# Block sums made in memory, two planner reserves, and adaptive sums by one-column products, in a planned two-layer decoder trunk

## The chip, the core and the metric

The kernel runs on one core of one Trainium2 chip. The metric is device time in microseconds (us) of one execution, the median of several. The engines are named as in the profile: PE is TensorE's matmuls, PEld its weight loads, DVE is VectorE, ACT is ScalarE, POOL is GpSimd, SP is SyncE, which here issues nearly all plain DMAs. POOL issues the DMAs that accumulate.

## The reference

Two layers of a hybrid decoder trunk on one sequence of 1024 tokens and 1024 channels, in float32, and a final RMSNorm:

```python
c_act = jax.nn.silu(c)
for l in range(DEPTH):
    ada = c_act @ w_ada[l] + b_ada[l]
    shift, scale, gate = jnp.split(ada, 3, axis=-1)
    h = rmsnorm(x, norm_g[l]) * (1.0 + scale[:, None, :]) + shift[:, None, :]
    p = h @ w_in[l]
    ...
    y = jnp.concatenate([y_m, y_r], axis=-1) @ w_out[l]
    x = x + gate[:, None, :] * y
return rmsnorm(x, final_g)
```

What stands at the "..." splits `p` among eight heads of 256 channels, four mLSTM heads (`y_m`) and four retention heads (`y_r`), each computed chunk by chunk and normalised. Two things matter for this change. The adaptive sums `c_act @ w_ada[l]` are products of one row of 1024 numbers with a 1024 x 3072 matrix. And `w_out` is 2048 x 1024: the kernel multiplies by it with seven block products in place of eight, for which it needs sums of blocks of `w_out` and of the heads' outputs.

## The kernel before

**A plan made at build time.** The program is first recorded as a list of operations on named buffers (`Program.record`), each with an assumed duration (`Program.cost`). Then `Program.simulate` plays it through: it takes the operations of each engine by due times, gives buffers to slots of their class, and lets DMAs go through one server one after another. `Program.order` does this for eight rounds, moves due times between them, and keeps the shortest plan. The final order of every engine's instructions, and which slot each buffer has, comes from there; on the chip each engine works through its own queue in that order and waits for semaphores. A reserve in the plan is time that the planner adds between two operations because the real time of one varies: `LATE` (1.5 us) after a DMA's landing for whoever uses it, `FAR` (5.0 us) in its place for buffers of the classes `q`, `kk`, `st` and `dm`.

**Numbers.** Every product of the large matrices is made of three TensorE matmuls on a high and a low float32r part (`mm3`: high x high, high x low, low x high). ACT makes the high part by a cast (`wH`, `hH`), DVE the low part by a subtraction (`wL`, `hL`). The weights' parts live in class `h`, which has nine slots of 128 x 512.

**The beginning (`beginning`).** SP loads, in an order that is pinned: half of `x` (eight tiles), then for each quarter `g` of the first layer's channels eight tiles `araw` of `w_ada` (128 rows of it, 256 columns each of shift and scale), with weights of the border in between, and the other half of `x` after the fourth quarter. `norm_rows` squares and scales the rows of `x`, TensorE transposes them (`pa<-ident,x`), and the result is copied to `xT`. `ada_part(g)` makes the adaptive sums of a quarter: TensorE multiplies the first `araw` tile by one column of `cact` (four products, one for each 128 columns), DVE multiplies the other seven by their column of `cact` and adds them into `aacc`, and TensorE adds up the partitions of `aacc` by four products with a column of ones, into the same bank. `finish_gsh` turns the bank into gain and shift, `gsh`; with these, `affine` makes `hH`, `hf` and `hL` of two tiles of `xT`, and the border's first products can run on them (`border_columns` on two column blocks, 512 columns a matmul, and `value_products`, 264 columns).

**The sums of blocks.** `weight_sums(l)` makes, for each of eight rows of blocks, four sums of two, three or four blocks of `w_out`: T1 = block 11 + 12, T2 = T1 + 22, T4 = T2 + 21, T3 = 12 + 22 (with the first digit for the half of the rows, the second for the half of the columns). It loads a block into a tile `fx` of class `h`, lets a DMA of POOL add the next block to it, stores the tile to `wdr`, adds again, and stores again. `early_job` and `late_job` do the same with the heads' outputs in `ydr`, into `fdr`. They are generators: one step of each is recorded after each pair of projections. `wdr` and `fdr` are read in `output`.

## Time and profile before

| | |
|---|---|
| median of three runs | 2096.32 us (2096.01 to 2097.2) |
| the profiled execution, its own time | 2095.88 us |
| its span, from the first to the last instruction | 2094.2 us |
| mean granted TensorE clock | 0.994 |
| DMA engines' mean use, HBM traffic | 229 GB/s, 322.16 MB read and 156.27 MB written |

The largest groups of the page, with their count, busy time, mean time of one, and the idle time of the engine just before them with what ended it:

```profile
L2068 PE MATMUL pp<-hH,wH 128*128 128x512 f32 x2416 | 958.2, 397 | 5.1 <-ACT hH L2068 2.8
L2068 PEld LDWEIGHTS pp<-hH,wL 128*128 128x128 f32 x2416 | 454.4, 188 | 106.9 <-DVE wL L2068 5.5
L2068 ACT CAST wH<-raw 128x512 fp32r<-128x512 f32 x515 | 315.5, 618 | 379.5 <-PE pp L2068 224.2
L2068 DVE TENSOR_TENSOR wL<-raw,wH 128x512 fp32r<-128x512 f32 x522 | 355.5, 685 | 106.6 <-ACT wH L2068 41.1
L2068 POOL DMA_DIRECT2D fx<-in_w_out_dram x64 | 56.7, 886 | 592.7 <-DMA wdr<-fx 188.8
```

All instructions have one line, L2068, since one loop at the end emits them in the planned order; so groups are told apart by their tiles. A matmul's duration here reaches into the next one (they are pipelined): what one costs is the distance from its start to the next one's. A fp32 product of one column, as the program writes it, shows as two matmuls.

### The profile page before, as it was taken

The numbers are of one execution on the slowest core, as the hardware profiler recorded it, in microseconds if no ns is written. First come the engines' busy times: TensorE is split into PE (matmuls) and PEld (weight loads), VectorE is DVE, ScalarE is ACT, GpSimd is POOL, SyncE is SP. The second block draws the span as 40 slices with busy tenths as digits, with TensorE's granted clock in tenths as the row PEclk, the third lists the DMA queues.
The fourth block names the chain that finished last, engine by engine and source line by source line (L and its number), as shares of the span: only waits on it lengthen the run. The fifth ranks groups of instructions, "written<-read, shape, count | busy, mean of one in ns | idle before, by whom it ended". The sixth has DMA issues, their size and how long they took to land.

```text
span 2094.2 us, 31188 instructions
## 1 busy us (share of the span) xinstructions
PE 2051.9 (98%) x9821; PEld 1705.8 (81%) x9821; DVE 1812.2 (87%) x3483; ACT 1139.4 (54%) x2124; POOL 206.1 (10%) x254
## 2 busy tenths in 40 slices
PE   6999999999999999999999999999999999999997
PEld 6888888778888888888888888888888888888886
DVE  7999999998887888894989989898978788888677
ACT  6755555456444444564666555566654434446544
POOL 0011110101001011011001000111010101110001
PEclk8999999999999999999999999999999999999999
DMA  9248676979796888999734699877768878989994
GB/s 302 80 138 222 186 214 177 254 229 265 228 269 191 246 257 233 272 318 339 231 117 117 174 238 256 232 219 202 228 195 241 232 227 226 271 250 301 333 319 149
DMA packets 508913, 480.55 MB, mean 229 GB/s; under 512 B 230706, under 2 KB 345146, under 8 KB 508748
## 3 DMA queue, kind: packets, MB, share of 16 engines
q1 hardware_dynamic: 493772, 451.29, 70.3%
q0 software_dynamic: 14976, 27.27, 7.9%
q8 instruction: 77, 1.26, 0.3%
q14 instruction: 88, 0.72, 0.1%
HBM read 322.16 MB, written 156.27 MB: 228 GB/s over the span
## 4 chain that ended last, share of the span: by engine, by line
PE 71%; DVE 13%; DMA 10%; issue 2%; SPq 2%; ACT 1%; POOL 0%; DVEq 0%; ACTq 0%; POOLq 0%
PE pp L2068 59%; PE pa L2068 12%; DVE wL L2068 3%; DVE acc L2068 2%; DVE x L2068 2%; DMA wdr<-fx 2%; SPq L2068 2%; DMA araw<-in_w_ada_dram 2%; DMA raw<-in_w_in_dram 1%; DVE raw L2068 1%; DVE rt L2068 1%; DMA fx<-in_w_out_dram 1%; DMA kk<-qdr 1%; DMA fdr<-fx 1%; DMA fx<-ydr 1%
## 5 line engine op out<-in xcount | busy, mean ns | idle before, releaser
L2068 PE MATMUL pp<-hH,wH 128*128 128x512 f32 x2416 | 958.2, 397 | 5.1 <-ACT hH L2068 2.8
L2068 PE MATMUL pp<-hL,wH 128*128 128x512 f32 x2416 | 957.0, 396 | 1.0 <-DVE hL L2068 1.0
L2068 PE MATMUL pp<-hH,wL 128*128 128x512 f32 x2416 | 955.4, 395 | 2.1 <-DVE wL L2068 1.9
L2068 PEld LDWEIGHTS pp<-hH,wL 128*128 128x128 f32 x2416 | 454.4, 188 | 106.9 <-DVE wL L2068 5.5
L2068 PEld LDWEIGHTS pp<-hH,wH 128*128 128x128 f32 x2416 | 454.4, 188 | 105.2 <-ACT wH L2068 2.9
L2068 PEld LDWEIGHTS pp<-hL,wH 128*128 128x128 f32 x2416 | 454.4, 188 | 101.6 <-DVE hL L2068 1.5
L2068 ACT CAST wH<-raw 128x512 fp32r<-128x512 f32 x515 | 315.5, 618 | 379.5 <-PE pp L2068 224.2
L2068 DVE TENSOR_TENSOR wL<-raw,wH 128x512 fp32r<-128x512 f32 x522 | 355.5, 685 | 106.6 <-ACT wH L2068 41.1
L2068 DVE SCALAR_TENSOR_TENSOR acc<-x,cols,acc 128x1024 f32<-128x1024 f32 x96 | 122.5, 1276 | 0.9 <-ACT acc L2068 0.7
L2068 POOL DMA_DIRECT2D fx<-in_w_out_dram x64 | 56.7, 886 | 592.7 <-DMA wdr<-fx 188.8
L2068 POOL TENSOR_TENSOR rsd<-va,mhalf 128x2 f32<-128x2 f32 x64 | 59.5, 930 | 562.1 <-DVE va L2068 494.4
L2068 PE MATMUL pa<-cf,q 128*128 128x258 f32 (+1 forms) x384 | 104.9, 380 | 1.9 <-DVE cf L2068 1.0
L2068 ACT ACTIVATE nd<-nd,nmu,rsd 128x256 f32<-128x256 f32 x117 | 65.3, 595 | 55.2 <-DVE nmu L2068 54.5
L2068 DVE TENSOR_TENSOR raw<-raw,raw 128x512 f32<-128x512 f32 x136 | 92.8, 684 | 0.6
L2068 PEld LDWEIGHTS pa<-q,kk 128*128 128x128 f32 x512 | 75.3, 191 | 8.7 <-issue 0.9
L2068 PEld LDWEIGHTS pa<-cf,q 128*128 128x128 f32 x384 | 69.1, 190 | 13.9 <-issue 1.8
L2068 PE MATMUL pa<-q,kk 128*128 128x128 f32 (+1 forms) x512 | 79.5, 301 | 0.5 <-DMA kk<-qdr 0.5
L2068 ACT CAST wH<-s 128x512 fp32r<-128x512 f32 x68 | 42.1, 619 | 67.7 <-PE pp L2068 35.0
L2068 DVE TENSOR_TENSOR hL<-yf,hH 128x512 fp32r<-128x512 f32 x90 | 60.7, 685 | 16.9 <-ACT hH L2068 15.3
L2068 ACT ACTIVATE yg<-yg,cols 128x512 f32<-128x512 f32 x63 | 45.5, 723 | 54.1 <-DVE yg L2068 53.5
L2068 PE MATMUL pa<-v,sd 128*128 128x258 f32 (+1 forms) x160 | 62.8, 393 | 2.1 <-ACT sd L2068 1.1
L2068 ACT CAST hH<-yf 128x512 fp32r<-128x512 f32 x89 | 53.6, 617 | 12.5 <-DMA yf<-fdr 4.9
(252 smaller groups left out, 2921.1 us busy)
## 6 DMA issues: line engine op xcount, KB each, us to landing
raw<-in_w_in_dram SPq DMA_DIRECT2D x280, 256.0 KB
araw<-in_w_ada_dram SPq DMA_DIRECT2D x96, 256.0 KB
fx<-in_w_out_dram POOLq DMA_DIRECT2D x64, 256.0 KB, 5.3
wdr<-fx SPq DMA_DIRECT2D x64, 256.0 KB
qdr<-acc SPq DMA_DIRECT2D x32, 512.0 KB
kk<-qdr SPq DMA_DIRECT2D x64, 256.0 KB
q<-qdr SPq DMA_DIRECT2D x64, 256.0 KB
ndr<-zt SPq DMA_DIRECT2D x128, 128.0 KB
```

The costliest lines, as they stand in the source:

```text
L2068: getattr(engines[op.eng], op.fn)(*[real(v) for v in op.a], **{n: real(v) for n, v in op.k.items()})
```

## The change

Three things are changed.

- The sums of blocks are made in memory: `sum_of` copies one block to its place in `wdr` or `fdr` (a DMA of SP, from memory to memory), and a DMA of POOL accumulates the other onto it there. T2 starts from a copy of T1, T4 from a copy of T2. Tiles `fx` are gone. `cost` now takes a DMA's size from its first operand where no operand is in SBUF.
- Two reserves: loads of wide `yg` tiles (class `X`) count as `far`; and a slot of class `h` is given away `LATE` after the end of a DMA among its users.
- `ada_part` makes the sums of the first two quarters from all eight `araw` tiles by products of one column, without `aacc`; the other two quarters stay as they were.

```diff
@@ record @@
-        op.far = isinstance(out, Ref) and out.buf.cls in ("q", "kk", "st", "dm")
+        op.far = isinstance(out, Ref) and (out.buf.cls in ("q", "kk", "st", "dm") or out.buf.name[:2] == "yg" and out.buf.cls == "X")
@@ cost @@
-            o = next(x for x in refs if not x.buf.dram)
+            o = next((x for x in refs if not x.buf.dram), refs[0])
...
+            k_accum = op.k.get("accum_op") is not None
...
+            if k_accum:
+                op.serve *= 1
@@ simulate @@
-                    slot_free[b.slot] = slot_last[b.slot].end
+                    slot_free[b.slot] = max(u.end + (self.LATE if u.bytes and b.cls == "h" else 0.0) for u in b.users)
@@ early_job @@
-            t = new("h", 512, "fx")
-            Q.dma_start(t, y_source(k, 0))
-            add_on(t, k, 1, "T1", k)
+            sum_of(fdr["T1"][k], y_source(k, 0), y_source(k, 1))
@@ late_job @@
-            t, u = (new("h", 512, "fx") for _ in range(2))
-            Q.dma_start(t, fdr["T1"][k])
-            Q.dma_start(u, y_source(k, 1))
-            add_on(t, k + KT, 1, "T2", k)
-            add_on(u, k + KT, 1, "T3", k)
-            add_on(t, k + KT, 0, "T4", k)
+            sum_of(fdr["T2"][k], fdr["T1"][k], y_source(k + KT, 1))
+            sum_of(fdr["T3"][k], y_source(k, 1), y_source(k + KT, 1))
+            sum_of(fdr["T4"][k], fdr["T2"][k], y_source(k + KT, 0))
@@ weight_sums @@
+    def sum_of(dst, one, two):
+
+        Q.dma_start(dst, one)
+        G.dma_start(dst, two, accum_op=ALU.add)
+
     def weight_sums(l):
         for k in range(KT):
-            for chain_ in (((None, 0, 0), ("T1", 0, 1), ("T2", 1, 1), ("T4", 1, 0)), ((None, 1, 1), ("T3", 0, 1))):
-                t = new("h", 512, "fx")
-                for name, kh, half in chain_:
-                    src = w_source(l, k + KT * kh, half)
-                    if name:
-                        G.dma_start(t, src, accum_op=ALU.add)
-                        Q.dma_start(wdr[name][k], t)
-                        yield
-                    else:
-                        Q.dma_start(t, src)
+            d = {n: wdr[n][k] for n in wdr}
+            for name, one, two in (("T1", w_source(l, k, 0), w_source(l, k, 1)), ("T2", d["T1"], w_source(l, k + KT, 1)),
+                                   ("T4", d["T2"], w_source(l, k + KT, 0)), ("T3", w_source(l, k, 1), w_source(l, k + KT, 1))):
+                sum_of(d[name], one, two)
+                yield
@@ ada_part @@
-            acc = new("F", 512, "aacc")
+            straight = (KT, KT, 1, 1)[g]
...
-            for i in range(4):
-                PE.matmul(pt[:, i:i + 1], raws[0][:, i * P:(i + 1) * P], cact[:, 0:1], start=i == 0, stop=False,
-                          skip_group_check=True)
-            ada_acc(acc, raws[1:], 1)
...
+            for kk in range(straight):
+                for i in range(4):
+                    PE.matmul(pt[:, i:i + 1], raws[kk][:, i * P:(i + 1) * P], cact[:, kk:kk + 1], start=kk == 0 and i == 0,
+                              stop=kk == KT - 1 and i == 3, skip_group_check=True)
+            if straight < KT:
+                acc = new("F", 512, "aacc")
+                ada_acc(acc, raws[straight:], straight)
+                for i in range(4):
+                    PE.matmul(pt[:, i:i + 1], acc[:, i * P:(i + 1) * P], ones, start=False, stop=i == 3,
+                              skip_group_check=True)
```

Since a planner sets the order, the diff alone does not tell where instructions stand. The first place is TensorE's queue near the first large matmul of the beginning (`pp<-hH,wH`, the border's columns on the first quarter). Of the kernel before, behind the transposes of `x`:

```order
L2068 MATMUL pa_251<-ident_74,rows_79 128x32
L2068 MATMUL pp_144<-ones_72,aacc_154 128x1 x4
L2068 MATMUL pp_294<-cact_113,araw_162 128x1 x4
L2068 MATMUL pp_326<-hH_314,wH_215 128x512
L2068 MATMUL pp_326<-hL_332,wH_215 128x512
L2068 MATMUL pp_326<-hH_314,wL_244 128x512
L2068 MATMUL pp_347<-hH_314,wH_235 128x512
L2068 MATMUL pp_294<-ones_72,aacc_260 128x1 x4
L2068 MATMUL pp_358<-cact_113,araw_253 128x1 x4
```

Of the change, at the same place; `pp_142` is the first quarter's bank, `pp_327` the second's, `pp_407` the third's:

```order
L2065 MATMUL pp_142<-cact_111,araw_134 128x1 x4
L2065 MATMUL pp_327<-cact_111,araw_162 128x1 x4
L2065 MATMUL pp_327<-cact_111,araw_169 128x1 x4
L2065 MATMUL pp_327<-cact_111,araw_178 128x1 x4
L2065 MATMUL pp_327<-cact_111,araw_185 128x1 x4
L2065 MATMUL pp_327<-cact_111,araw_197 128x1 x4
L2065 MATMUL pp_327<-cact_111,araw_211 128x1 x4
L2065 MATMUL pp_327<-cact_111,araw_221 128x1 x4
L2065 MATMUL pp_327<-cact_111,araw_233 128x1 x4
L2065 MATMUL pp_407<-cact_111,araw_265 128x1 x4
L2065 MATMUL pp_418<-hH_340,wH_226 128x512
L2065 MATMUL pp_418<-hL_352,wH_226 128x512
```

All products of the second quarter, and the first of the third, have moved ahead of the first large matmul; the eight groups of the first quarter stand ahead of these rows, among the transposes. The second place is SP's queue at the end of the border's first half, where `bv` (the value projection) is stored to `v0dr`. Of the kernel before:

```order
L2068 DMA raw_612<-in_w_in_dram 128x512
L2068 DMA v0dr_815<-bv_800 128x512
L2068 DMA v0dr_831<-bv_812 128x512
L2068 DMA raw_836<-in_w_in_dram 128x512
L2068 DMA raw_843<-in_w_in_dram 128x512
```

Of the change (`wdr<-in_w_out` is a copy of a block of `w_out`, `wdr<-wdr` a copy of a sum on which the next one builds):

```order
L2065 DMA wdr_806<-in_w_out_dram 128x512
L2065 DMA wdr_846<-wdr_642 16x4096
L2065 DMA wdr_863<-wdr_648 16x4096
L2065 DMA v0dr_878<-bv_854 128x512
L2065 DMA v0dr_891<-bv_881 128x512
L2065 DMA wdr_900<-wdr_659 16x4096
L2065 DMA wdr_912<-wdr_667 16x4096
L2065 DMA raw_927<-in_w_in_dram 128x512
```

The copies of layer 0's weight sums, which were spread over the whole layer, now stand here, ahead of and between the stores of `bv` and the loads of `raw`. The third place is POOL's queue behind the second `rs` (the row norms of `x`'s second half). Of the kernel before:

```order
L2068 TENSOR_TENSOR rs_586<-s_578,mhalf_70 128x4
L2068 MEMSET T_458_1103 128x512
L2068 DMA fx_1194<-in_w_out_dram 128x512
L2068 MEMSET T_464_1291 128x512
L2068 DMA fx_1194<-in_w_out_dram 128x512
L2068 AFFINE_SELECT dm_1287<-dm_1287 128x256
```

Of the change, from the 19th accumulate behind `rs` on (`T` is a tile of the gate chain, which the first heads need):

```order
L2065 DMA wdr_1036<-in_w_out_dram 128x512
L2065 DMA wdr_1048<-in_w_out_dram 128x512
L2065 MEMSET T_456_1182 128x512
L2065 DMA wdr_1065<-in_w_out_dram 128x512
L2065 DMA wdr_1085<-in_w_out_dram 128x512
L2065 DMA wdr_1192<-in_w_out_dram 128x512
L2065 DMA wdr_1200<-in_w_out_dram 128x512
L2065 DMA wdr_1255<-in_w_out_dram 128x512
L2065 DMA wdr_1266<-in_w_out_dram 128x512
L2065 DMA wdr_1295<-in_w_out_dram 128x512
L2065 MEMSET T_462_1407 128x512
```

Twenty accumulates stand ahead of the first `MEMSET T`, where there was none.

More of the change, by code (lines that the diff above doesn't have):

```diff
@@ L1567, in y_half @@
         return yr, g
-    def add_on(t, k, half, name, row):
-        G.dma_start(t, y_source(k, half), accum_op=ALU.add)
-        Q.dma_start(fdr[name][row], t)
     def early_job(l, ks):
@@ L1771, in ada_part @@
             raws = load_ada(g)
-            acc = new("F", 512, "aacc")
+            straight = (KT, KT, 1, 1)[g]
             was, prog.stream = prog.stream, "sums"
             pt = bank("p")
-            for i in range(4):
-                PE.matmul(pt[:, i:i + 1], raws[0][:, i * P:(i + 1) * P], cact[:, 0:1], start=i == 0, stop=False,
-                          skip_group_check=True)
-            ada_acc(acc, raws[1:], 1)
-            for i in range(4):
-                PE.matmul(pt[:, i:i + 1], acc[:, i * P:(i + 1) * P], ones, start=False, stop=i == 3,
-                          skip_group_check=True)
+            for kk in range(straight):
[8 more added lines that the diff above has]
+                              skip_group_check=True)
             prog.stream = was
```

## Prediction

> **What bounds the kernel now.** I began with the first part of the profile's page and then asked for the busy time by stages.
>
> ```profile
> span 2094.2 us, 31188 instructions
> PE 2051.9 (98%) x9821; PEld 1705.8 (81%) x9821; DVE 1812.2 (87%) x3483; ACT 1139.4 (54%) x2124; POOL 206.1 (10%) x254
> ...
> 12.20:43.90 31.70, 26.38 (x133) 23.64 (x133) 28.87 (x65) 18.67 (x43) 1.02 (x1) 0.78 1.09 356
> 43.90:2081.80 2037.90, 2025.30 (x9688) 1682.00 (x9688) 1776.16 (x3401) 1108.28 (x2052) 201.66 (x243) 1.00 0.78 228
> 2081.80:2094.20 12.40, 0.01 (x1) 0.00 (x0) 6.26 (x13) 5.39 (x12) 2.54 (x4) 0.62 0.45 169
> ```
>
> (A stage's row has its length, then the busy time of PE, PEld, DVE, ACT and POOL, the granted clock of TensorE, and the DMA engines' share and GB/s.) The reader is to see that TensorE is the bound. Between 43.9 and 2081.8 us it is busy for 2025.30 of 2037.90 us, so 12.6 us is all that a better order, freer buffers or quicker sums can give back there. The 12.2 us ahead of these stages (waiting for the first adaptive weights) and the 12.4 us behind the last matmul are not touched. There remains the beginning, 12.2 to 43.9: TensorE idle for 5.3 of 31.7 us, at a mean clock of 0.78. So each part of the change is priced by what it does to TensorE: work added, idle time before it, and the clock that it is granted.
>
> **The products of one column.** TensorE's rows of the beginning, and one of VectorE:
>
> ```profile
> 12.21 1.84 PE L2068 MATMUL pp<-cact,araw 128*128 128x1 f32 x8 [9.58 <-DMA araw<-in_w_ada_dram]
> 14.16 6.58 PE L2068 MATMUL pa<-ident,x 128*128 128x128 f32 x32
> 20.66 0.24 PE L2068 MATMUL pa<-ident,rows 32*128 32x32 f32 x1
> ...
> 21.95 1.03 PE L2068 MATMUL pp<-cact,araw 128*128 128x1 f32 x8
> 25.81 0.80 PE L2068 MATMUL pp<-hH,wH 128*128 128x512 f32 x1 [2.83 <-ACT hH L2068]
> ...
> 30.63 1.84 PE L2068 MATMUL pp<-cact,araw 128*128 128x1 f32 x8
> 32.34 0.77 PE L2068 MATMUL pp<-hL,wH 128*128 128x512 f32 x1
> ...
> 38.91 1.03 PE L2068 MATMUL pp<-cact,araw 128*128 128x1 f32 x8
> 39.80 0.37 PE L2068 MATMUL pa<-vwH,hH 128*128 128x264 f32 x1
> ...
> 40.13 0.29 PE L2068 MATMUL pa<-vwH,hL 128*128 128x264 f32 x1
> 40.25 0.28 PE L2068 MATMUL pa<-vwH,hH 128*128 128x264 f32 x1
> ...
> 41.45 0.39 PE L2068 MATMUL pp<-hH,wL 128*128 128x512 f32 x1
> 41.68 0.39 PE L2068 MATMUL pp<-hH,wH 128*128 128x512 f32 x1
> ```
>
> ```profile
> 27.48 0.75 DVE L2068 SCALAR_TENSOR_TENSOR aacc<-araw,cact,aacc 128x512 f32<-128x512 f32 x1
> ```
>
> The four products that the program writes for one `araw` tile are eight matmuls in the trace. From its start to the next row's, such a group takes 32.34 - 30.63 = 1.71 us at half clock and 39.80 - 38.91 = 0.89 at full clock. A 512-column matmul takes 0.23 (41.45 to 41.68), a 264-column one 0.12 (40.13 to 40.25). The 32 transposes of `x` took 20.66 - 14.16 = 6.5.
>
> Before, each of the first two quarters took two groups: one on `araw`, one on `ones`. After, each takes eight. That adds 12 groups, 12 x 0.89 = 10.7 us of TensorE work at full clock, and takes 14 operations of at most 0.75, about 10 us, from VectorE. What VectorE held up is seen at 25.81: the first quarter's sums were through TensorE before 21.95, and the first large matmul still waited until 25.81.
>
> But TensorE works through its queue in order, and the order of the change puts all eight groups of the first quarter, all eight of the second and one of the third ahead of the first large matmul. Their data does not space them out: SP issues these loads in the same order, and VectorE was at the second quarter's last multiply-add by 27.48. So 17 groups now stand where four stood between the first weights and the first large matmul.
>
> How long they take hangs on the clock (same columns as above; PEclk is the third number from the end).
>
> ```profile
> 20.00:22.00 2.00, 1.87 (x17) 1.59 (x15) 1.67 (x6) 2.00 (x7) 0.00 (x0) 1.00 1.10 349
> 22.00:24.00 2.00, 0.98 (x9) 0.90 (x9) 2.00 (x5) 1.04 (x9) 0.00 (x0) 0.77 1.10 348
> 24.00:26.00 2.00, 0.19 (x1) 0.19 (x1) 2.00 (x7) 1.06 (x2) 0.00 (x0) 0.50 1.10 349
> ...
> 30.00:32.00 2.00, 2.00 (x11) 2.00 (x11) 2.00 (x8) 0.07 (x1) 0.00 (x0) 0.50 1.08 374
> 32.00:34.00 2.00, 2.00 (x9) 1.81 (x8) 2.00 (x4) 2.00 (x3) 0.00 (x0) 0.50 1.09 360
> 34.00:36.00 2.00, 2.00 (x11) 2.00 (x11) 1.56 (x3) 1.79 (x5) 0.00 (x0) 0.50 1.11 352
> 36.00:38.00 2.00, 2.00 (x10) 1.65 (x10) 1.58 (x3) 0.00 (x0) 0.00 (x0) 0.81 1.08 346
> ```
>
> The clock was full behind the solid run of transposes and fell at about 23.1 (0.77 over 22 to 24), though TensorE had been busy for 1.87 of the two microseconds before 22; most of that was groups of one column. From 30 to 32 it was busy without a gap, on such groups, and stayed at 0.50. It rose at about 36.8 (0.81 over 36 to 38), 4.4 us after the dense matmuls began at 32.34. I read: one-column products keep TensorE busy and do not earn it the clock. The group at 12.21 took the same 1.84 as the one at 30.63, so the start is at half clock too, whatever the column shows ahead of its first record.
>
> The Trainium skill speaks against this: "TensorE: Matmul & The Clock Gate", Part 1, has the gate watch how busy TensorE was in a window of about 3.4 us, whatever the instructions, and open after one busy window. By that rule the change would end near 2093.5 (a rival below); the row from 30 on disagrees with it for products of one column.
>
> So 17 groups at 1.71 are 29.1 us. Behind the transposes I grant 3 us of full clock, as before (full at 21.95 by that group's 1.03, lost at 23.1): they do 3.4 groups, which saves 2.8. With 0.4 for the small transposes, the first large matmul starts at 12.2 + 6.5 + 29.1 - 2.8 + 0.4 = 45.4 us, not at 25.8. Until 43.9 us the kernel before did this:
>
> ```profile
> L2068 PE MATMUL pp<-hL,wH 128*128 128x512 f32 x6 | 3.3, 553 | 1.0 <-DVE hL L2068 1.0
> L2068 PE MATMUL pp<-hH,wH 128*128 128x512 f32 x6 | 3.2, 540 | 2.8 <-ACT hH L2068 2.8
> L2068 PE MATMUL pa<-vwH,hH 128*128 128x264 f32 x9 | 3.2, 354 | 0.0
> ...
> L2068 PE MATMUL pp<-hH,wL 128*128 128x512 f32 x6 | 2.8, 472 | 0.0
> L2068 PE MATMUL pa<-vwL,hH 128*128 128x264 f32 x8 | 2.8, 353 | 0.0
> L2068 PE MATMUL pa<-vwH,hL 128*128 128x264 f32 x8 | 2.8, 353 | 0.0
> ```
>
> That is 18 x 0.23 + 25 x 0.12 = 7.2 us at full clock, all still to do in the change. Of the one-column groups one was left before, and three are left after: 2 x 0.89 = 1.8. With 45.4 - 43.9 = 1.5, the change is 10.5 us behind when its dense work begins, and it begins that at half clock: 4.4 us of it, as from 32.34 on before, lose about 2.0. Sum: **12.5 us later**. Nothing takes it back: from 43.9 on TensorE has hardly a gap, and VectorE's 10 us serve a queue that does not end last. Bounds: 9 if the clock rises early, 16 if the one-column groups between the first dense ones hold it down for a few microseconds more.
>
> **The sums in memory.** Each sum becomes a copy from memory to memory on SP's queue and an accumulate into memory on POOL's, in place of a load, an accumulate and a store through a tile of class `h`. For the weights, 32 loads and 64 stores become 64 copies, and the 64 accumulates stay; for the outputs, 24 loads and 28 stores become 28 copies. So SP issues 56 fewer, and the nine `h` tiles are all left to the splits of the weights. Since the weight sums of layer 0 no longer wait for a tile, they move to the border, ahead of the gate chain: on SP between the stores of `bv` and loads of `raw`, on POOL ahead of `MEMSET T`. The rows nearest to their worth are TensorE's own waits after the beginning, and what an accumulate into a tile took:
>
> ```profile
> PE pp L2068 <- ACT wH L2068: 2.3, 2, 1.6
> PE pa L2068 <- DVE cf L2068: 2.3, 4, 0.7
> PE pp L2068 <- DVE wL L2068: 1.9, 4, 0.9
> ```
>
> ```profile
> DMA to landing us min/median/max: 3.7/5.7/9.1
> ```
>
> None of TensorE's waits is put down to a sum. Two, on `wH` and `wL` (2.3 + 1.9 = 4.2 us), are on tiles of class `h`; freeing these tiles could remove them, and a new order will make others. I take half, **2.1 us gained**, nearest to those rows. Bounds: 6 gained, half of the 12.6 us; 4 lost, since copies and accumulates that write memory are not in the trace and SP holds the loads of `raw` behind copies that wait for them.
>
> **The two reserves.** The planner adds 1.5 us before it gives an `h` tile away whose last user was a DMA; but `fx` was the only tile of that class that a DMA touched, and it is gone. So this one does nothing: 0. The other gives the loads of wide `yg` tiles 5.0 us in place of 1.5 in the plan. It moves VectorE's multiplies of `yg`, which TensorE never waited for in the rows above: 0, inside the bounds of the last part.
>
> **Sum.** The profiled execution took 2095.88 us with a span of 2094.2, 0.44 under the median of the three runs, 2096.32. 2095.9 + 12.5 - 2.1 = **2106.3 us**.
>
> **The rivals.**
>
> *One-column products earn the clock.* Say it is full from 19.7 us on. By then 3.3 groups and 9 transposes (at 6.5 / 32 = 0.20) are done; 13.7 groups at 0.89, 23 transposes at 0.10 and 0.4 follow: the first large matmul is at 34.6 us. The change is then 9.0 - 9.3 = -0.3 us behind and has no cold start: 2095.9 - 0.3 - 2.1 = 2093.5, not slower. For it: TensorE would be busy without a break. Against it: 30 to 32 us. It decides if PEclk is 1.00 over the second quarter's groups.
>
> *The burst on POOL and SP holds up the gate chain.*
>
> ```profile
> 48.80 1.29 POOL L2068 TENSOR_TENSOR rs<-s,mhalf 128x4 f32<-128x4 f32 x1 [35.22 <-DVE sm L2068]
> ```
>
> ```profile
> L2068 DVE COPY T<-lfq x4: 407/416/417, 151.2 to 1183.5; 4x512 f32<-4x512 f32 x4
> ```
>
> POOL has 27 accumulates between `rs` (50.1) and the second `MEMSET T`, and VectorE first wants `T` at 151.2, or 163.7 when 12.5 us late: it decides from (163.7 - 50.1) / 27 = 4.2 us for each. At 4.6 VectorE, and TensorE behind it, stand for some 11 us: 2117. For it: landings of 3.7 to 9.1 us if they ran one by one. Against it: within a round of eight they do not depend on each other.
>
> *The middle gains most of its idle time:* 9 of the 12.6 us, in place of 2.1: 2095.9 + 12.5 - 9 = 2099.4. For it: nine tiles free for good. Against it: waits on `cf`, for one, have nothing to do with them.
>
> **How the numbers follow.** Forecast 0.70 (its own range 2099 to 2114), clock rival 0.14, burst rival 0.09, quiet middle 0.07. A measurement of this kernel tells about 0.2%, 4.2 us, from no change: below 2092.1 is faster, above 2100.5 slower. Slower: 0.68 of the forecast, the burst, and 0.02 of the quiet middle: 0.79. Faster: 0.05, a third of the clock rival. Same: 0.16. The range, 2096 to 2115, leaves out most of the clock and burst rivals, about 0.2.
>
> **What would show it.** Right, if in the profile after the first 512-column matmul starts between 42 and 48 us, if PEclk is 0.50 over most of 26 to 45 us and groups of eight take 1.7 there, and if PE's idle time from then to the last matmul is 8 to 17 us. Wrong, if groups of eight take 0.9 from 20 us on; if the first large matmul stands before 37; or if long PE waits on `T`, `raw` or `wH` appear after 60 us.

## The result, and the profile after

| | before | after |
|---|---|---|
| median of 15 runs each | 2097.36 us (2092.99 to 2100.15) | 2106.5 us (2098.62 to 2109.48) |
| ratio | 1 | 1.0033, 95% interval 1.0023 to 1.0043 |
| the profiled execution, its own time | 2095.88 us | 2100.24 us |
| its span | 2094.2 us | 2098.5 us |

The change makes the kernel slower by a third of a percent. The profiled execution is one of the quicker ones of the changed kernel: its fifteen times lie in two groups, five from 2098.6 to 2100.9 and ten from 2103.7 to 2109.5.

From the page of the changed kernel, the span and the engines, then the busy time by stages (columns as before: length; busy PE, PEld, DVE, ACT, POOL; PEclk; DMA share; GB/s):

```profile
span 2098.5 us, 31082 instructions
PE 2063.5 (98%) x9917; PEld 1724.5 (82%) x9917; DVE 1805.9 (86%) x3468; ACT 1145.8 (55%) x2125; POOL 214.1 (10%) x254
...
43.90:2086.00 2042.10, 2031.05 (x9743) 1692.89 (x9741) 1781.66 (x3399) 1121.52 (x2070) 209.63 (x243) 1.00 0.77 220
```

96 more matmuls, as counted. TensorE's idle time from 43.9 us to its last matmul is 2042.10 - 2031.05 = 11.05 us, little less than the 12.6 of before. But it is made of something else. The same view of both kernels, cut where the new wait stands, first before:

```profile
50.00:1050.00 1000.00, 991.21 (x4752) 822.85 (x4751) 890.04 (x1742) 546.22 (x1009) 106.25 (x126) 1.00 0.78 228
1050.00:1100.00 50.00, 50.00 (x268) 42.56 (x268) 44.14 (x86) 30.22 (x52) 1.01 (x1) 1.00 0.35 116
1100.00:2080.00 980.00, 976.19 (x4624) 809.77 (x4623) 834.61 (x1553) 526.62 (x980) 93.20 (x116) 1.00 0.81 234
```

and after:

```profile
50.00:1050.00 1000.00, 996.45 (x4806) 830.70 (x4805) 892.98 (x1741) 553.43 (x1019) 123.20 (x136) 1.00 0.79 226
1050.00:1100.00 50.00, 42.51 (x207) 34.73 (x206) 37.01 (x77) 27.34 (x53) 13.31 (x17) 0.90 1.05 271
1100.00:2080.00 980.00, 980.00 (x4670) 816.92 (x4669) 846.15 (x1571) 537.60 (x995) 73.12 (x92) 1.00 0.74 213
```

Idle time in the first layer falls from 8.8 to 3.6 us and in the second from 3.8 to 0.0. Between them, where there was none, stand 7.5 us, with the clock at 0.90 and the DMA engines full (1.05 for 0.35). The waits of TensorE from 50 to 2080 us (total, how often, longest) name it:

```profile
PE pa L2065 <- DVE dg L2065: 6.7, 1, 6.7
PE pp L2065 <- DVE cols L2065: 1.7, 1, 1.7
PE pp L2065 <- DVE hf L2065: 0.8, 1, 0.8
PE pp L2065 <- ACT wH L2065: 0.6, 1, 0.6
```

`dg` is the diagonal of the row norms between the layers. VectorE makes it from `rs`, and POOL makes `rs` from `s`. VectorE had `s` at 1075.5 (its row `s<-pa` starts at 1075.37 and takes 0.13). POOL's timeline:

```profile
1061.26 0.84 POOL L2065 DMA_DIRECT2D wdr<-in_w_out_dram  x1 [1.48 <-issue]
1071.55 2.50 POOL L2065 DMA_DIRECT2D wdr<-in_w_out_dram  x3 [9.45 <-DMA wdr<-wdr]
1080.14 0.83 POOL L2065 DMA_DIRECT2D wdr<-in_w_out_dram  x1 [6.10 <-issue]
1081.90 0.82 POOL L2065 DMA_DIRECT2D wdr<-in_w_out_dram  x1 [0.92 <-issue]
1082.45 1.35 POOL L2065 TENSOR_TENSOR rs<-s,mhalf 128x4 f32<-128x4 f32 x1
```

`rs` starts 7 us late. Ahead of it in POOL's queue stand five accumulates of layer 1's weight sums. The first, in the row at 1071.55, waited for a copy into `wdr` to land. The last two, at 1080.14 and 1081.90, did not: by the trace's record of landings their copies were there at 1073.47 and 1074.10, and the view names no releaser for them ("issue"). They start 0.3 us after the first and the second accumulate of the row at 1071.55 landed (1079.84 and 1081.59). In none of the fourteen traces does POOL start an accumulate while three earlier ones are under way, and in this one 51 of 104 start 0.25 to 0.4 us after the third before them has landed. So with three under way POOL holds back the next accumulate, and with it whatever stands behind it; what sets the number three is not shown. In the kernel before no accumulate stood near this `rs`:

```profile
1073.47 1.01 POOL L2068 TENSOR_TENSOR rs<-s,mhalf 128x4 f32<-128x4 f32 x1 [39.77 <-DVE s L2068]
1114.64 0.53 POOL L2068 MEMSET T<- 128x512 f32 x1 [40.17 <-ACT hH L2068]
1124.19 0.90 POOL L2068 DMA_DIRECT2D fx<-in_w_out_dram  x1 [9.02 <-PE pp L2068]
```

The trace's clock record shows half clock from 1079.81, 1.9 us into TensorE's wait, to 1090.05, 5.5 us past its end.

The beginning, TensorE's timeline and then stages of two microseconds:

```profile
24.38 17.35 PE L2065 MATMUL pp<-cact,araw 128*128 128x1 f32 x98
41.59 0.77 PE L2065 MATMUL pp<-hH,wH 128*128 128x512 f32 x1
42.16 0.63 PE L2065 MATMUL pp<-hL,wH 128*128 128x512 f32 x1
```

```profile
26.00:28.00 2.00, 2.00 (x20) 2.00 (x20) 1.24 (x12) 0.07 (x1) 0.00 (x0) 1.00 1.09 363
28.00:30.00 2.00, 2.00 (x14) 2.00 (x13) 1.99 (x4) 2.00 (x4) 0.00 (x0) 0.63 1.09 375
30.00:32.00 2.00, 2.00 (x11) 2.00 (x11) 1.97 (x5) 0.05 (x1) 0.00 (x0) 0.50 1.07 375
36.00:38.00 2.00, 2.00 (x11) 2.00 (x11) 0.00 (x0) 0.00 (x0) 0.00 (x0) 0.50 1.10 349
44.00:46.00 2.00, 2.00 (x13) 1.90 (x11) 0.00 (x0) 0.27 (x1) 0.00 (x0) 0.61 1.04 395
46.00:48.00 2.00, 2.00 (x18) 2.00 (x18) 1.76 (x7) 0.77 (x2) 0.00 (x0) 1.00 0.53 182
```

TensorE is busy without a gap and at half clock from 28.5 to 45.57. The first large matmul starts at 41.59.

How far a kernel is behind at a place can be read from the instructions that both traces have. Taken here: the VectorE, ACT and POOL instructions of groups that have equal counts in both, the k-th of one against the k-th of the other, and the median difference over the stretch of 100 us that begins at the time given. The changed kernel is +9.8 us against before at 100 us, +0.2 at 900, +11.3 at 1100 and +4.7 at 2000. So: about 10 us lost at the start, as many regained in the first layer, 11 lost at the wait for `rs`, and 6.6 regained in the second layer. Of the 16 us regained, 9.0 are idle time that is gone (8.8 to 3.6 and 3.8 to 0.0); where the rest comes from is not shown.

### The profile page after: what moved, and what is told of

It reads as the page before. It is cut to its first block, busy times and chain, and to the rows that moved or that the text cites. A ratio compares the mean times of both kernels' runs of the same rounds, so it can differ in the third digit from the quotient of the medians.

```text
span 2098.5 us, 31082 instructions
## 1 busy us (share of the span) xinstructions
PE 2063.5 (98%) x9917; PEld 1724.5 (82%) x9917; DVE 1805.9 (86%) x3468; ACT 1145.8 (55%) x2125; POOL 214.1 (10%) x254
## 4 chain that ended last, share of the span: by engine, by line
PE 83%; DMA 1%; DVE 1%; issue 1%; ACT 0%; POOL 0%; SPq 0%; DVEq 0%; POOLq 0%; ACTq 0%
PE pp L2065 70%; PE pa L2065 14%; DMA wdr<-wdr 0%; SPq L2065 0%; POOL wdr L2065 0%; DMA kdr<-x 0%; DVE xr L2065 0%; DMA ndr<-zt 0%; ACT hH L2065 0%; DVE o L2065 0%; ACT hf L2065 0%; DVE wL L2065 0%; ACT tmp L2065 0%; DVE x L2065 0%; POOL rs L2065 0%
## 5 line engine op out<-in xcount | busy, mean ns | idle before, releaser
L2065 PEld LDWEIGHTS pa<-cf,q 128*128 128x128 f32 x384 | 69.8, 189 | 11.3
L2065 ACT COPY ca<-pp 128x512 f32<-128x512 f32 x68 | 39.7, 584 | 67.0 <-PE pp L2065 66.9
L2065 ACT COPY cb<-pp 128x512 f32<-128x512 f32 x67 | 39.0, 582 | 60.8 <-PE pp L2065 60.6
L2065 POOL TENSOR_SCALAR_AFFINE_SELECT dm<-dm 128x256 f32<-128x256 f32 (+1 forms) x64 | 51.0, 814 | 192.5 <-DMA dm<-mdr 184.4
L2065 POOL DMA_DIRECT2D wdr<-in_w_out_dram x64 | 53.3, 867 | 150.1 <-issue 75.7
```

Of the source, the lines that this page charges most:

```text
L2065: getattr(engines[op.eng], op.fn)(*[real(v) for v in op.a], **{n: real(v) for n, v in op.k.items()})
```

## The experiments

Theory A was that the products cost some 10 us at the start. Theory B: sums in memory quiet the middle, and their place in POOL's queue costs the wait at 1077. The rivals are in the expectations. Every ratio is against runs of the kernel before on the same chip, with its 95% interval. The columns at the right give how far the profiled execution is behind that of the kernel before (us, at 100, 900, 1100 and 2000 us).

| run | median us (before) | ratio | 100 | 900 | 1100 | 2000 |
|---|---|---|---|---|---|---|
| the change | 2106.5 (2097.36) | 1.0033 (1.0023 to 1.0043) | 9.8 | 0.2 | 11.3 | 4.7 |
| after_again | 2106.52 (2098.72) | 1.0032 (1.0019 to 1.0044) | 11.5 | 2.2 | 12.2 | 5.6 |
| cols_alone | 2121.63 (2099.67) | 1.0100 (1.0079 to 1.0121) | 12.6 | 14.4 | 15.8 | 17.8 |
| cols_reserves | 2112.7 (2100.84) | 1.0065 (1.0053 to 1.0077) | 12.3 | 15.7 | 15.9 | 16.7 |
| sums_alone | 2107.05 (2099.67) | 1.0035 (1.0022 to 1.0048) | 13.9 | 7.0 | 16.0 | 9.5 |
| sums_held | 2100.47 (2099.67) | 1.0001 (0.9989 to 1.0012) | 0.3 | -2.9 | 3.6 | 0.6 |
| l1_held | 2099.87 (2099.67) | 0.9999 (0.9986 to 1.0012) | 18.5 | 9.5 | 9.9 | 4.5 |
| wsum_l1 | 2100.99 (2098.72) | 1.0009 (0.9999 to 1.0019) | 10.6 | -0.6 | -0.2 | -4.5 |
| wide_l1 | 2090.68 (2098.72) | 0.9960 (0.9947 to 0.9973) | 10.3 | 2.0 | 2.5 | -0.5 |
| reserves | 2090.48 (2098.72) | 0.9957 (0.9943 to 0.9971) | -0.1 | -3.5 | -3.1 | -5.9 |
| yg_alone | 2100.6 (2100.84) | 1.0004 (0.9995 to 1.0012) | -0.2 | 6.0 | 6.3 | 6.8 |
| no_yg | 2115.2 (2100.84) | 1.0075 (1.0059 to 1.0090) | 18.5 | 13.3 | 25.6 | 19.9 |
| first_wide | 2099.2 (2100.84) | 0.9994 (0.9984 to 1.0003) | 4.7 | 1.4 | 1.8 | 1.4 |

Two cautions. The profiled execution is not always a typical one: it is the fastest of its kernel in cols_alone (2113.63 us), wsum_l1 (2091.34) and after_again (2101.17), and the slowest in wide_l1 (2095.2). And each variant has a plan of its own. No run has the same kernel with another plan, so what a new order does by itself is not separated from what a part does, except where the orders are said to be the same. no_yg, which differs from the change by one reserve alone, lies 0.0042 or 9 us above it, and whether that is the reserve or the order stays open; so a difference of that size is no proof of what a part does.

### The parts by themselves, and the wait on rs

The kernel before with the products only:

```diff
-ada_acc(acc, raws[1:], 1)
...
+straight = (KT, KT, 1, 1)[g]
...
+for kk in range(straight):
+    for i in range(4):
+        PE.matmul(pt[:, i:i + 1], raws[kk][:, i * P:(i + 1) * P], cact[:, kk:kk + 1], ...)
```

> The kernel before, with only the one-column products of the first two quarters in place of the multiply-adds (sums through tiles, no reserves). Theory A (the products cost about 10 us at the start, and nothing else of the change comes from them): first 512-column matmul near 41.6 us as in the changed kernel, about 10 us over the kernel before on the same chip (some 2107 us, ratio 1.004 to 1.006), the waits of the middle as before (PE idle some 12 us between the first large matmul and the last), no wait on dg near 1077 us. Rival (the other order that the products bring is also what quiets the middle): idle time there falls to 5 us and the time is 2098 to 2102.

Measured: 2121.63 us, ratio 1.0100. Both theories missed it. The beginning is that of the change (first large matmul at 41.97, half clock from 28.27 to 45.34), but nothing is regained behind it: 12.6 us behind at 100 us, 17.8 at 2000, and that in the fastest of six executions, 8 us under the median. What the others lose beyond that, no profile shows. TensorE's waits from 50 to 2080 us:

```profile
PE pp L2071 <- ACT wH L2071: 4.7, 2, 2.7
PE pa L2071 <- DVE st L2071: 4.0, 3, 2.2
PE pp L2071 <- DVE wL L2071: 3.3, 6, 1.0
PE pa L2071 <- DVE T L2071: 2.8, 2, 1.9
```

With the tiles `fx` still there, `wH` and `wL` cost 8.0 us instead of 4.2. In the changed kernel they cost 1.0.

The sums in memory (and both reserves) without the products:

```diff
-straight = (KT, KT, 1, 1)[g]
+straight = (1, 1, 1, 1)[g]
```

> The changed kernel with the multiply-adds of the kernel before: sums in memory and both reserves, no extra products. Theory B (sums in memory gain about 15 us in the middle, and give about 10.6 back in one wait on rs near 1077 us, 6.7 of idle time and 10 us at half clock): first 512-column matmul near 22 to 26 us, one PE wait of 4 to 8 us near 1070, time about 5 us under the kernel before (2090 to 2095). Rival (as the prediction priced it: 2 us gained, plus the wait): 2102 to 2108.

Measured: 2107.05 us; the rival's number, though not by its reasons. The wait on `dg` is there (6.6 us), and the middle regains 6.9 us by 900 and 6.5 behind 1100, as theory B has it. The loss that it did not have is at the start: 13.9 us by 100 us. TensorE's waits from 38 to 200 us:

```profile
PE pa L2065 <- DVE vwL L2065: 3.6, 1, 3.6
PE pp L2065 <- DVE cb L2065: 3.5, 1, 3.5
PE pa L2065 <- DVE T L2065: 2.9, 1, 2.9
PE pa L2065 <- DVE g L2065: 2.0, 2, 1.1
```

This is the burst rival of the prediction only in part. The wait on `vwL` ends at 42.42, before the first copy is issued (49.52), so it belongs to the new order and not to the burst. The one on `cb` fits the rival's half on SP: the chain ahead of it runs through a store `v0dr<-bv`, issued at 91.41 among the copies, that takes 11.9 us; the four such stores of layer 0 took 2.0 to 2.1 us before. The rival's half on POOL does not show: the second `MEMSET T` ran at 122.83, and TensorE's wait on `T` ends at 185.42, behind VectorE's own work. In the changed kernel these stores take 5.2 to 8.4 us and TensorE does not wait for `cb`; that the products, which make everything behind them late, hide it is argued, not shown.

The sums of layer 1 held back in the plan to the time at which the program records them (`nom`, the plan's running sum of TensorE's work), in that layer's own work:

```diff
+op.ready = op.nom if op.held else 0.0
...
+op.held = isinstance(out, Ref) and out.buf.name[:3] == "wdr" and self.nom > 1000
```

> The changed kernel, with the weight sums of layer 1 held in the plan until that layer's own work begins, so that none stands ahead of the row norms' rs on POOL near 1077 us; up to there the order is the same. Theory B: rs runs within 2 us of s, PE waits for dg under 1 us, no half clock there; about 10 us less than the changed kernel (2090 to 2097 where that has 2100 to 2107). Rival 1 (the stall there is only the place where a clock window or the load on memory shows): another wait or half-clock stretch of several us appears and the time stays within 3 us of the changed kernel. Rival 2 (sums held later hold up layer 1 in turn): long PE waits behind 1400 us.

Measured: 2099.87 us, ratio 0.9999 where the change has 1.0033. Up to 990 us every engine's order is that of the change. The mechanism of theory B holds: TensorE waits for nothing between 1050 and 1100 us, and the clock stays full there. POOL's timeline has

```profile
1083.37 1.01 POOL L2067 TENSOR_TENSOR rs<-s,mhalf 128x4 f32<-128x4 f32 x1 [40.36 <-DVE s L2067]
1124.61 0.53 POOL L2067 MEMSET T<- 128x512 f32 x1 [40.23 <-ACT hH L2067]
```

and VectorE's

```profile
1084.41 0.69 DVE L2067 TENSOR_TENSOR dg<-ident,rs 128x512 f32<-128x512 f32 x1 [1.12 <-POOL rs L2067]
```

The profile after 1100 us has no long wait either, so rival 2 falls. The two intervals don't meet; 0.0034 of 2098 us is **7.1 us for the wait on `rs`**, under the 10 that the theory had. In the profiles it is 10.7: between 900 and 1100 us the change loses 11.1 us and this kernel 0.4. The profile of this run shows one thing more, at the start, which is taken up below.

Both layers' sums held in that way, without the products (against l1_held):

```diff
-op.held = isinstance(out, Ref) and out.buf.name[:3] == "wdr" and self.nom > 1000
+op.held = isinstance(out, Ref) and out.buf.name[:3] == "wdr"
-straight = (KT, KT, 1, 1)[g]
+straight = (1, 1, 1, 1)[g]
```

> Sums in memory and both reserves, without the extra products, and the weight sums of both layers held in the plan to the place where the program writes them. Theory A and B together (no products: 0 at the start; no accumulates ahead of rs; the middle quiet): 13 to 17 us under the kernel before, 2080 to 2085, PE idle under 6 us between 50 and 2080 us. Rival (the middle's gain came from doing the sums early, in the border): 2091 to 2097.

Measured: 2100.47 us, 18 us above the theory's middle, and above the rival's range too. The start is as before (0.3 us at 100) and there is no wait on `rs`. But held sums regain only 3.2 us by 900, and then one wait takes that away:

```profile
930.64 0.39 PE L2067 MATMUL pp<-hH,wL 128*128 128x512 f32 x1
935.16 0.79 PE L2067 MATMUL pp<-hH,wH 128*128 128x512 f32 x1 [4.13 <-ACT hf L2067]
935.75 0.63 PE L2067 MATMUL pp<-hL,wH 128*128 128x512 f32 x1
```

4.1 us of idle time, and from 933.84 half clock for 6.83 us. The chain ahead of it runs through VectorE's multiplies of `yg`; what makes them late was not tried.

The changed kernel once more:

> The changed kernel itself, once more. Theory (two things set its time: the wait on rs near 1077 us, in every execution, and when the clock comes back behind the first products, near 45 us in some executions and near 57 us in others): median 2103 to 2109 with times in two clusters some 6 us apart; in the profile PE waits 4 to 8 us for dg near 1077 to 1085 us again. Rival (the wait near 1077 us was chance in one execution): no such wait in this profile.

Measured: 2106.52 us; the wait on `dg` is there again (7.5 us, and half clock for 6.83 us around its end). Its times, 2101.2 to 2110.7, spread as before, though without a clear gap.

### The clock at the start

The clock record of the trace says when the full clock came behind the transposes, when it was lost, and when it came back:

| kernel | full from | half from | full again | first large matmul |
|---|---|---|---|---|
| before | 19.68 | 23.09 | 36.75 | 25.81 |
| the change | 21.67 | 28.50 | 45.57 | 41.59 |
| after_again | 21.37 | 28.20 | 45.26 | 41.66 |
| cols_alone | 21.45 | 28.27 | 45.34 | 41.97 |
| l1_held | 23.43 | 26.85 | 57.57 | 44.76 |
| wide_l1 | 22.92 | 91.19 | 94.60 | 36.17 |

Every stretch in it, but for the last one, is a whole number of 3.41 us (6.83 is two, 17.07 five, 30.72 nine); such a unit is called a window here. In l1_held, whose order up to there is the change's, it was nine windows of half clock instead of five. TensorE's rows of l1_held show what ran in them (distance to the next row's start: 1.57 us for eight one-column products behind 48.12, at half clock):

```profile
47.91 0.42 PE L2067 MATMUL pa<-vwH,hL 128*128 128x264 f32 x1
48.12 1.70 PE L2067 MATMUL pp<-ones,aacc 128*128 128x1 f32 x8
49.69 0.57 PE L2067 MATMUL pa<-vwH,hH 128*128 128x264 f32 x1
50.05 1.70 PE L2067 MATMUL pp<-cact,araw 128*128 128x1 f32 x8
51.61 0.57 PE L2067 MATMUL pa<-vwL,hH 128*128 128x264 f32 x1
```

Two groups of one-column products stand between the first dense ones. In l1_held the windows end at 47.33, 50.74 and 54.15, and each holds some of these products; the first without any is the next, and at its end, 57.57, the full clock comes back. In the change's profiled execution the window from 42.16 to 45.57 was dense but for its last 0.6 us. All in all l1_held has 15.4 us more of half clock (full 1.8 later, half 13.65 longer), 7.7 us of work; it is 18.5 us behind at 100 us, the change 9.8. That this makes the two groups of times is argued, not shown, since only profiled executions have a clock record: the four quickest runs of l1_held (2095.5 to 2097.4) have a mean clock of 0.993, and of the six slowest five have 0.989 or 0.990.

To test what earns the clock, the products were widened, in the same order (against l1_held):

```diff
-PE.matmul(pt[:, i:i + 1], raws[kk][...], cact[:, kk:kk + 1], ...)
+PE.matmul(pt[:, 64 * i:64 * i + 64], raws[kk][...], cact[:, kk:kk + 1].to_broadcast([P, 64]), ...)
```

> The changed kernel with layer 1's weight sums held as in the run before, and each one-column product made 64 columns wide (the same column of the activations 64 times; of the result one column in 64 is used). The order of the instructions is the same. Theory A (a product of one column keeps TensorE busy but does not earn it the clock; what counts is how much it streams): groups of four take 0.5 us at full clock all through 22 to 45 us, first 512-column matmul near 34 to 36 us, no half clock behind 22 us, 9 to 16 us less than with one column (2084 to 2091 where that has 2100). Rival (the gate looks at busy time alone, and the half clock comes from something else in the beginning, as the transfers at full load): clock and time as with one column, within 3 us.

Measured: 2090.68 us, ratio 0.9960. Stages of two microseconds:

```profile
30.00:32.00 2.00, 2.00 (x20) 2.00 (x19) 1.99 (x5) 0.93 (x3) 0.00 (x0) 1.00 1.08 379
34.00:36.00 2.00, 2.00 (x21) 2.00 (x19) 1.73 (x5) 0.00 (x0) 0.00 (x0) 1.00 1.04 335
...
100.00:102.00 2.00, 0.43 (x1) 0.44 (x2) 1.97 (x6) 1.92 (x4) 0.00 (x0) 0.86 1.03 247
```

The transfers are as dense as before, the matmuls as many and in the same order; with 64 columns each the clock stays full from 22.92 to 91.19, and the first large matmul starts at 36.17, just above the 34 to 36 of theory A. TensorE's order is that of l1_held. The gain of 0.0039, 8 us, is just under its 9 to 16. Between 100 and 200 us the kernel is 10.3 behind all the same, since TensorE now waits for `cols` (1.6 us), `ca` (3.2) and `T` (2.6) of the border, and loses the clock there for three windows. That layer 0's sums, which still stand ahead of these, cause the waits was not tried. This profile is of the slowest execution: the other five lie between 2089.9 and 2091.2, with a mean clock of 0.996 or 0.997 for its 0.995.

### The reserves, and which sums

```diff
-op.far = ... out.buf.cls in ("q", "kk", "st", "dm")
+op.far = ... (out.buf.cls in (...) or out.buf.name[:2] == "yg" and out.buf.cls == "X")
-slot_free[b.slot] = slot_last[b.slot].end
+slot_free[b.slot] = max(u.end + (self.LATE if u.bytes and b.cls == "h" else 0.0) for u in b.users)
```

> The kernel before with the two reserves alone (1.5 us before a tile of class h is given away behind a DMA, 5.0 us for the loads of the wide yg tiles); sums through tiles, multiply-adds as before. Theory: no step of the result comes from them, within 3 us of the kernel before (2094 to 2100). Rival (the reserve on class h, with the tiles of the sums still there, is what quiets the middle): PE idle between 50 and 2080 us falls from 12 to under 7 us and the time by 5 us or more.

Measured: 2090.48 us, ratio 0.9957: faster by 8.2 us than before, which neither forecast had whole. The time is the rival's, its sign in the profile is not: TensorE's idle time from 50 us to its last matmul is 10.2 us for 12.6 before, not under 7. Its half clock at the start is a window shorter (10.24 us in place of 13.65), but so it is in yg_alone, which has the order of the kernel before up to 288 us, and at 100 us neither is more than 0.2 us ahead. By 900 us it is 3.5 us ahead; no single wait stands out.

With the first of the two lines alone:

> The kernel before with one reserve only, 5.0 us in the plan for the loads of the wide yg tiles; the other reserve, on tiles of class h, left out. The two together gave 8.2 us. Theory (the reserve on h gives it, since in the kernel before nine fx tiles of that class have loads and stores of their own): within 3 us of the kernel before (2095 to 2101). Rival (the yg reserve, the only one of the two that has anything to act on in the changed kernel): 2088 to 2093.

Measured: ratio 1.0004, 0.9995 to 1.0012. The time is as the theory has it: without the reserve on class `h` the gain is gone. That class is where `fx` is, and the reserve is meant to keep the planner from handing a slot on before the DMA has surely landed. That reserve by itself was not run, and whether it gains by its slack or by the other order that comes with it is not shown.

The change without the reserve on `yg`:

```diff
-or out.buf.name[:2] == "yg" and out.buf.cls == "X"
```

> The changed kernel without the reserve on the wide yg tiles (that on class h has no tile to act on there). Theory (as priced in the prediction: 0 for it): within 3 us of the changed kernel (2103 to 2110). Rival (the reserve pays some 8 us in the changed kernel as it may in the kernel before): 2112 to 2117.

Measured: 2115.2 us, ratio 1.0075 against 1.0033. The theory falls by time, and the rival's range has it. But of the 15.3 us that it is behind the change at 2000 us, the two profiles compared directly, 8.3 are there at 100 us: in this execution the full clock lasted one window (25.07 to 28.48) and came back at 48.96. The rest, 7 us, comes in the first layer and at the wait for `dg` (8.1 us). How much of it is the reserve and how much a new order's luck stays open.

Products and reserves, sums through tiles (the diffs of cols_alone and reserves together):

> The kernel before with the one-column products of the first two quarters and both reserves; sums through tiles. Without the reserves that took 2121, the reserves alone 2090. Theory (the parts add up, products +22 and reserves -8): 2110 to 2115. Rival (the products alone cost the 10 to 16 us of the start, and the rest of the +22 was waits on h tiles that the reserves remove too): 2099 to 2107.

Measured: 2112.7 us. The parts add up here. Its stages, to be held against the change's:

```profile
50.00:1050.00 1000.00, 985.86 (x4744) 819.71 (x4743) 882.00 (x1721) 543.64 (x1013) 115.73 (x126) 1.00 0.78 226
...
1100.00:2080.00 980.00, 975.45 (x4654) 810.91 (x4653) 838.61 (x1568) 533.07 (x986) 93.43 (x112) 1.00 0.81 233
```

14.1 and 4.6 us of idle time, against 3.6 and 0.0 in the change. This kernel and l1_held differ only in how the sums are made (with the hold, and with the `h` reserve, which has nothing to act on once `fx` is gone): 1.0065 against 0.9999, **14 us for sums in memory beside the products**. Without the products, reserves against sums_held (which holds both layers' sums), it is 0.9957 against 1.0001, 9 us the other way. Both figures hold for these plans; the second is of the size that a new order alone may bring.

The sums of the outputs through tiles again, those of the weights in memory and held as in l1_held:

```diff
-sum_of(fdr["T1"][k], y_source(k, 0), y_source(k, 1))
+t = new("h", 512, "fx")
+Q.dma_start(t, y_source(k, 0))
+add_on(t, k, 1, "T1", k)
...
```

> The changed kernel with layer 1's weight sums held, and the sums of the outputs y through tiles of class h again (weights' sums still in memory). Theory C (the early weight sums, which leave the nine h tiles to the splits of the weights for nearly all of a layer, quiet the middle): within 4 us of the same kernel with all sums in memory (2096 to 2104). Rival (the 28 sums of the outputs are what blocks the tiles): waits on wH, wL and st come back and it takes 8 to 15 us more (2108 to 2115).

Measured: 2100.99 us, inside theory C: with the weights' sums alone in memory, the gain is there.

Last, a try at a better version: both reserves, sums through tiles, products for the first quarter only, 64 columns wide:

```diff
+straight = (KT, 1, 1, 1)[g]
...
+PE.matmul(pt[:, 64 * i:64 * i + 64], raws[kk][...], cact[:, kk:kk + 1].to_broadcast([P, 64]), ...)
```

> The kernel before with both reserves, sums through tiles, products in place of multiply-adds for the first quarter only, and all one-column products on the activations made 64 columns wide. Theory (the wide products keep the clock, and half of them fit beside the loads): the half clock between 25 and 36 us goes, first 512-column matmul near 28 us, 2083 to 2090, under the reserves alone (2090). Rival (the beginning is bound by the loads, so that PE waits for them instead): the clock stays full but PE waits 4 us or more for wH, hH or vwL before 60 us, and the time is 2090 to 2095.

Measured: 2099.2 us, worse than the reserves alone. The rival's waits came: 2.4 us for `vwL` and 1.6 for `hH` before 52 us. Its full clock did not: half clock from 30.86 to 37.69 and again from 47.93. The time lies above both ranges. The versions that beat both kernels are **reserves** (2090.48) and **wide_l1** (2090.68).

## Why the prediction was right, and where not

The time (2106.3 forecast, 2106.5 measured) and the sign were right. That they agree to 0.2 us is luck. The sum was made for the profiled execution, as 10.4 us on top of that of the kernel before; the profiled execution of the changed kernel (2100.24) is 4.4 us longer, so there the sum is 6 us too high, and the medians differ by 9.1. Of its terms, the products were about right; the sums in memory were not. Of the signs, the half clock and the 1.7 us of a group came, the first large matmul stood just outside its range, and the idle time fell inside 8 to 17 us, but for another reason than the one given.

- **The products.** Right in kind: 96 matmuls, at half clock, ahead of the first large one. The forecast for that was 45.4 us and the trace has 41.59, just under the range of 42 to 48 that was to show it. The term that failed is the full clock granted around the transposes, as before. Before it was one window of 3.41 us, and in the change two, 6.83; 3.4 us more at double speed do another 3.4 us of the queue, and the first product started 0.25 us sooner (11.96 for 12.21): 45.4 - 3.4 - 0.25 = 41.75. The dense part's half clock was 4.0 us for 4.4 foreseen. The 12.5 us were 9.8 in that profile, inside the bounds of 9 to 16. With these corrections the term would be some 8.5; a wait on `cols` of 1.7 us at 97.78, which the kernel before does not have, is about the rest (an estimate). Where the clock came back late, the profile of l1_held shows 18.5, beyond them. The bound named the cause (one-column groups between the first dense ones) and gave it too little.
- **What earns the clock.** Right, and shown by wide_l1. The Trainium skill, "TensorE: Matmul & The Clock Gate", Part 1, has a free-running window of 3413 ns, and the trace agrees: every stretch of the clock record, but for the last one, is a multiple of 3.41 us. Its rule that the gate watches how busy TensorE was, and that one busy window opens it, is not what this kernel shows, as far as the profile's busy time is what the gate watches: TensorE was busy for 2.00 of every 2.00 us from 30 to 44 and stayed at 0.50, and the same queue with 64 columns kept 1.00.
- **The sums in memory, 2.1 us gained.** Mis-sized, and in two directions. The middle was worth far more: 9.6 us regained in the first layer and 6.6 in the second, over the bound of 6. The step took half of two waits on `h` tiles, and capped the rest at the idle time of the page; it saw the waits that were there, not those that the late start would meet with tiles of `fx` (cols_alone). Against that stands a wait that the sum did not have, 11 us in the profile and 7.1 by l1_held. Together they left 5 us, near the 2.1 by luck.
- **The burst rival** (0.09) had the mechanism, accumulates ahead of a small POOL operation for which TensorE waits, and the wrong place. It was priced at the gate chain in layer 0, where the changed kernel waits for `T` 0 us in one profile and 2.2 in the other, and not at every operation of POOL behind the burst. `rs` between the layers stands behind layer 1's. In layer 0 the 27 accumulates took 63.5 us (60.54 to 124.02), 2.4 us each with up to three under way, where 4.2 would have been needed: neither one by one nor all eight at a time, as the prediction weighed it.
- **The quiet middle** (0.07) happened too, 16 us and not 9. As rivals, both were kept apart from the forecast, though nothing excluded that they come together.
- **The reserves, 0.** In the change, the one on `h` has nothing to act on; that step stands. On the kernel before, the two reserves together come with 8 us, and without the one on `h` these are gone. The one on `yg` isn't shown to be 0.

## What to carry to other kernels

An operation that is cheap on its engine can be dear by where it stands: before a DMA is given to a queue that also computes, look for every small operation of that engine that others wait for, here one `pow` of 1 us behind accumulates that waited for a copy and then, three being under way, for each other. Price TensorE work by the clock it will be granted, and where very narrow products stand between dense ones, widen them or move them out. And test the parts of a change alone and together: the sums in memory, in the plans tried, were worth 14 us beside the products and cost 9 without them, and of the parts tried by themselves the one that paid was the pair of reserves in the plan. Where a planner remakes the order for each variant, try the same part under more than one order before you believe a gain of a few us.

## What was not expected of the hardware

- POOL starts no fourth accumulate (256 KB each) while three are under way: 0 of 104 do in each of fourteen traces, and in the change 51 of 104 start within 0.4 us of the landing of the third before them.
- Very narrow products lose the full clock even in an unbroken run: it was granted for 3.41 or 6.83 us behind or among the transposes, and then lost with TensorE 2.00 of 2.00 us busy. The same order got five or nine windows of half clock in different executions.
- One idle stretch of 4.1 us (sums_held) or 6.7 us (the change) brought 6.83 and 10.24 us of half clock, which began within the wait. In both cases 5.5 us of it fell on work after the wait (935.16 to 940.67, 1084.58 to 1090.05) and cost half of that, 2.7 us; so the wait cost some 1.7 and 1.4 times itself, an estimate.
- An accumulate of 256 KB from memory onto memory landed 4.3 to 11.1 us after its issue, median 7.3; the one into a tile, before, 3.7 to 9.1, median 5.7. The loads differ: 83 of 104 accumulates started with no other under way before, 32 after.
